# Turned data moves by another engine's DMA queue, its writes half a step later

## The chip, the cores and the metric

The kernel runs on one core of one Trainium2 chip. The metric is device time in microseconds; the kernel before takes 981.33 us (median of 3 runs, 980.38 to 981.82).

## The reference

A decoder trunk of two layers over 256 rows of 2048 columns, in float32. Each layer normalises its rows and multiplies them by one wide input matrix. Its columns are the queries, keys and values of two kinds of attention, the queries of a cross-attention into 256 memory rows, and a gate. The heads' outputs are multiplied by `silu(gate)` and sent through an output matrix; the input is added.

```python
h = rms_norm(x, norm_g) @ w_in
# layer 0: latent attention (8 heads), block attention (8 heads), memory attention (4 heads)
# layer 1: windowed attention with sinks (16 heads), dilated attention (6), memory attention (4)
y = jnp.concatenate([o_a, o_b, o_m], axis=-1) * jax.nn.silu(gate)
x = x + y @ w_out
```

A last RMS norm follows. With 256 rows every causal attention has two blocks of 128 queries.

## The kernel before, in words

Weights stream from memory in pieces of 128 partitions by up to 1024 elements (two row blocks of up to 512 columns). SyncE issues each piece's transfer into one of four `raw` tiles (line 329). ScalarE (ACT in the profile) writes its rounded part `hi` (L413) and VectorE (DVE) the rest `lo`; there are four buffers of each. TensorE (PE) makes each product in three matmuls, x-high by `hi`, x-high by `lo`, x-low by `hi` (L568 to L570), into a ring of four PSUM tiles. A piece is two half-steps of six matmuls. After each half-step `run_bg` (L475) advances all running background generators by one `yield`, so a `yield` means half a step later. A budget of VectorE work per half-step makes non-urgent generators skip a turn when it is spent. `ensure(i + AHEAD, True)` (L538) splits weights three pieces ahead of PE.

The instruction order on every engine's queue is fixed by this written order. An instruction that has to wait holds everything behind it on its engine.

Products come with rows on partitions, and attention needs them turned. This takes two steps. VectorE transposes blocks of 32 by 32; the rest of the turn is done by writing the tile to memory and reading it back with another order of blocks. Two generators do this:

- `g_land` (L652) for two `wide` tiles of projected data: rotary products on GpSimd where needed (L635 to L650), transposes into a `big` tile, write to `wd` (L667), read back (L671), then the parts are handed on.
- `g_turn` (L844) for a tile `P` of softmax probabilities: transpose, write to `pd` (L850), read back (L853). `g_causal_T` calls it for causal heads; `g_mem_T` (L883) runs two of them side by side for memory heads and counts their half-steps itself.

All these transfers stand on SyncE's queue, between the weights. A read waits for the landing of its write. Heads are taken from a queue at most every fourth half-step; each goes through split, scores, softmax, turn and the product with the values, and ends in a block of `y` (a high and a low part, `put_y`). The output projections (`wo00` to `wo13`) read these blocks; if one has not yet been written in the order, the background runs on until it has.

Of the kernel before, what the change touches and what calls it, by code (L numbers as in the profile page):

```python
# [206 lines left out]
def body(ctx, tc, xr, xT, memT, memr, wall, gains, fing, sinks, consts, out):  # L207
    nc = tc.nc
# [286 lines left out]
    def mmtile():  # L495
        if len(mmring) == 4:
            mmring.popleft()["force"]()
        mmring.append({})
        return ps.tile([128, 512], F32, name="mm", tag="mm", bufs=4), mmring[-1]
# [120 lines left out]
    def rope_rows(W, n, s0, s1, kind, t):  # L620

        tab, m, w, k = {"d": (cst, 8, 32, 128), "c": (lay, 4, 16, 128), "r": (lay, 8, 8, 256)}[kind]
        per = 32 // w
        if kind == "r":
            v = W[:, 0:128 * n].rearrange("p (b g h i) -> p b g h i", b=4, h=2, i=8)[:, :, 2 * s0:2 * s1]
            x1, x2 = v[:, :, :, 0], v[:, :, :, 1]
            g = 2 * (s1 - s0)
        else:
            v = W[:, 0:128 * n].rearrange("p (b g i) -> p b g i", b=4, i=w)[:, :, per * s0:per * s1, 0:m]
            g = per * (s1 - s0)  # L630
        cs, sn = (tab[:, 2 * k * i + k * t:2 * k * i + k * t + k].rearrange("p (b g i) -> p b g i", b=4, i=m)
                  [:, :, 0:g] for i in range(2))
        e = wtile("e", 512, 2)
        A, B = (e[:, 256 * i:256 * i + 4 * g * m].rearrange("p (b g i) -> p b g i", b=4, i=m) for i in range(2))
        mul, add = (lambda o, a, b: nc.gpsimd.tensor_tensor(o, a, b, op=OP.mult)), OP.add  # L635
        if kind == "r":
            e = wtile("e", 512, 2)
            C, E = (e[:, 256 * i:256 * i + 4 * g * m].rearrange("p (b g i) -> p b g i", b=4, i=m) for i in range(2))
            mul(A, x1, cs)
            mul(B, x2, sn)  # L640
            mul(C, x2, cs)
            mul(E, x1, sn)
            nc.gpsimd.tensor_tensor(x1, A, B, op=OP.subtract)
            nc.gpsimd.tensor_tensor(x2, C, E, op=OP.add)  # L644
        else:
            lo, hi = slice(0, m // 2), slice(m // 2, m)
            mul(A, v, cs)
            mul(B[:, :, :, lo], v[:, :, :, hi], sn[:, :, :, lo])
            mul(B[:, :, :, hi], v[:, :, :, lo], sn[:, :, :, hi])
            nc.gpsimd.tensor_tensor(v, A, B, op=OP.add)  # L650

    def g_land(Ws, n, ropes, done, L=None):  # L652

        for k in ropes:
            for t in range(2):
                rope_rows(Ws[t], n, *k, t)
            yield
        while L is None and not big.free:
            yield
        L = L or big.get()  # L660
        w = 128 * n
        for t in range(2):
            vec.transpose(L[:, w * t:w * t + w], Ws[t][:, 0:w])
            wide.put(Ws[t])
        yield
        d = wds.get()
        nc.sync.dma_start(d[0:256 * w].rearrange("(t p f) -> p t f", t=2, p=128),  # L667
                          L[:, 0:2 * w].rearrange("p (t f) -> p t f", t=2))
        for _ in range(5):
            yield  # L670
        nc.sync.dma_start(L[:, 0:2 * w].rearrange("p (g f) -> p g f", g=8),  # L671
                          d[0:256 * w].rearrange("(g p f) -> p g f", g=8, p=128))
        wds.put(d)
        for _ in range(6):
            yield
        land = {"t": L, "n": n}
        done([Part(land, s, n) for s in range(n)])

    def rows(kinds, done, r=None):


        n = len(kinds)
        n0 = n - kinds.count("g")
        ropes = [(kinds.index(k), kinds.rindex(k) + 1, k) for k in "dcr" if k in kinds]

        def evac(cur):
            Ws = []
            while len(wide.free) < 2:
                yield
            for t in range(2):  # L690
                Ws.append(wide.get())
                o = laid_out(Ws[t], n)
                src = rows_of(cur[t][:, 0:128 * n], n)
                if n0:
                    copy(o[:, :, 0:n0], src[:, :, 0:n0], r, t)
                if n0 < n:
                    nc.scalar.activation(o[:, :, n0:n], src[:, :, n0:n], AF.Tanh, scale=hx[:, t:t + 1])
            yield
            if n0 < n:
                for t in range(2):  # L700
                    o, src = laid_out(Ws[t], n), rows_of(cur[t][:, 0:128 * n], n)
                    vec.tensor_scalar(o[:, :, n0:n], o[:, :, n0:n], 1.0, hx[:, t:t + 1], op0=OP.add, op1=OP.mult)
                    vec.tensor_tensor(o[:, :, n0:n], o[:, :, n0:n], src[:, :, n0:n], op=OP.mult)
                yield
            launch(g_land(Ws, n, ropes, done))
        return evac
# [35 lines left out]
    def g_turn_x(x):  # L742

        for _ in range(4):
            yield
        while len(wide.free) < 2:
            yield
        Ws = [wide.get(), wide.get()]
        for t in range(2):
            copy(laid_out(Ws[t], 4), rows_of(x[:, 512 * t:512 * t + 512], 4), None, t)  # L750
            yield
        yield from g_land(Ws, 4, [], XT.append, x)
# [91 lines left out]
    def g_turn(P, W, n):  # L844

        vec.transpose(P[:, 0:128 * n], W)
        yield
        d = pds.get()
        c = d[0:128 * 128 * n]
        nc.sync.dma_start(c.rearrange("(p f) -> p f", p=128), P[:, 0:128 * n])  # L850
        for _ in range(4):
            yield
        nc.sync.dma_start(P[:, 0:128 * n].rearrange("p (a f) -> p a f", a=4),  # L853
                          c.rearrange("(a p f) -> p a f", a=4, p=128))
        pds.put(d)
        for _ in range(5):
            yield

    def g_causal_T(P, r, out):

        while not pw.free:
            yield
        w = pw.get()
        (_, p0), (_, p1) = cuts3(P)
        nc.scalar.activation(laid_out(w, 3)[:, :, 1:3], p1, AF.Copy, scale=r[:, 1:2])
        vec.tensor_scalar(laid_out(w, 3)[:, :, 0:1], p0, r[:, 0:1], None, op0=OP.mult)
        yield
        pw.put(w)
        yield from g_turn(P, w[:, 0:384], 3)
        while not ptp.free:  # L870
            yield
        PT = ptp.get()
        hi, lo = PT[:, 0:256], PT[:, 256:512]
        p = P.rearrange("p (a s j) -> p s a j", a=4, s=3)
        parts = [v.rearrange("p (s a j) -> p s a j", a=4, s=2) for v in (hi, lo)]
        out.append((hi, lo, p[:, 2], PT))
        nc.scalar.activation(parts[0], p[:, 0:2], AF.Copy)  # L877
        yield
        vec.tensor_tensor(parts[1], p[:, 0:2], parts[0].bitcast(F32), op=OP.subtract)
        yield  # L880
        yield

    def g_mem_T(P, r, out):  # L883

        gs = []
        for t in range(2):
            while not pw.free:
                yield
            w = pw.get()
            if t:  # L890
                nc.scalar.activation(w[:, 0:256], P[t][:, 0:256], AF.Copy, scale=r[:, 1:2])
            else:
                vec.tensor_scalar(w[:, 0:256], P[t][:, 0:256], r[:, 0:1], None, op0=OP.mult)
            yield
            pw.put(w)
            gs.append(g_turn(P[t], w[:, 0:256], 2))
            next(gs[t])
        for i in range(11):
            for g in gs:
                next(g, None)  # L900
            if i < 10:
                yield
        while not (ptp.free and spl.free):
            yield
        hi, lo = ptp.get(), spl.get()
        p = [P[t][:, 0:256].rearrange("p (a s j) -> p s a j", a=4, s=2) for t in range(2)]
        parts = [v.rearrange("p (s t a j) -> p t s a j", t=2, s=2, a=4) for v in (hi, lo)]
        out.append((hi, lo))
        for t in range(2):
            nc.scalar.activation(parts[0][:, t], p[t], AF.Copy)  # L910
        yield
        for t in range(2):
            vec.tensor_tensor(parts[1][:, t], p[t], parts[0][:, t].bitcast(F32), op=OP.subtract)
        yield
        yield
# [229 lines left out]
    w = spl.free[0][:, 0:128]  # L1145
    vec.memset(w.bitcast(F32), 1.0)
    for i in range(10):
        a = ones if i < 7 else w
# [370 lines left out]
    n = len(plan[-1][1].sizes)  # L1519
    for t in range(2):  # L1520
        p, slot = mmtile()
        slot["force"] = lambda: None
        for i in range(n):
            ensure(npieces - n + i)
            hi, lo = splits[npieces - n + i]
            for h in range(2):
                x = y1(2 * i + h)
                w = slice(512 * h, 512 * h + 512)
# [58 lines left out]
```

## Time and profile before

| what | value |
|---|---|
| median of 3 runs | 981.33 us |
| the profiled execution's own time | 980.83 us |
| its span (first to last instruction) | 979.0 us |
| PE busy | 960.9 us |
| ACT busy | 584.4 us |
| weights issued on SyncE, 512 KB each | 309 |
| landed data: writes and reads | 34 and 34 |
| probabilities: writes and reads | 54 and 54 |

Busy time of an engine does not include waiting, or issuing transfers. SyncE's queue appears as SPq, issues on ScalarE's queue as ACTq. Idle time of an engine that is not the bottleneck costs nothing, so the table is read together with the waits.

### The profile page before, as it was taken

To read this page: it belongs to the slowest core of one execution; us is meant where nothing else is said; L and a number is where in the kernel's file an instruction comes from. 1 tells how busy PE (TensorE), PEld (TensorE's weight loads), DVE (VectorE), ACT (ScalarE), POOL (GpSimd) and SP (SyncE) were. 2 spreads that over 40 slices of the span, in tenths; PEclk is the share of its full clock that TensorE was granted. 3 is DMA by queue.
4 is the path that set the end of the run, shared out by engine and by line. 5 is a ranking of instruction groups with operands and counts; after the bars stand their busy time and mean duration, and the time that the engine had idled before them with its cause. 6 is when DMAs were issued, how large, how long until landed. Compare 5 with 4: busy or idle time off the path is not lost.

```text
span 979.0 us, 13403 instructions
## 1 busy us (share of the span) xinstructions
PE 960.9 (98%) x4541; PEld 806.7 (82%) x4541; DVE 665.8 (68%) x1174; ACT 584.4 (60%) x1060; POOL 95.5 (10%) x159
## 2 busy tenths in 40 slices
PE   9999998999999999999999999999999999999996
PEld 7888876888888888888888888888888988898885
DVE  6746767777767656776656655867968767676743
ACT  7766645676756646665656544656757765655541
POOL 0001221000011011010000000010202111001410
PEclk9999998999999999999999999999999999999999
DMA  9888966997677787887987867696777878699832
GB/s 336 324 272 268 317 203 222 329 305 233 216 255 212 236 259 227 262 306 250 325 267 274 268 205 236 201 282 215 233 273 240 300 223 267 198 309 305 296 108 86
DMA packets 136692, 248.26 MB, mean 254 GB/s; under 512 B 38960, under 2 KB 80176, under 8 KB 136624
## 3 DMA queue, kind: packets, MB, share of 16 engines
q1 hardware_dynamic: 135904, 246.59, 76.7%
q10 hardware_dynamic: 720, 0.82, 0.2%
q8 instruction: 35, 0.57, 0.2%
q14 instruction: 33, 0.27, 0.1%
HBM read 216.05 MB, written 31.33 MB: 253 GB/s over the span
## 4 chain that ended last, share of the span: by engine, by line
PE 84%; DVE 0%; ACT 0%; POOL 0%; issue 0%; ACTq 0%; DVEq 0%
PE mm L568 25%; PE mm L569 25%; PE mm L570 25%; PE at L951 2%; PE at L942 2%; PE at L946 1%; PE mm L1533 1%; PE mm L1532 1%; PE mm L1531 1%; PE at L955 1%; PE at L1069 0%; DVE big L202 0%; ACT big L1505 0%; DVE st L202 0%; POOL wide L644 0%; ACT wide L616 0%
## 5 line engine op out<-in xcount | busy, mean ns | idle before, releaser
L202 DVE TENSOR_TENSOR lo<-raw,hi 128x1024 fp32r<-128x1024 f32 (+3 forms) x331 | 398.9, 1211 | 187.0 <-ACT hi L413 184.3
L413 ACT ACTIVATE hi<-raw 128x1024 fp32r<-128x1024 f32 (+3 forms) x329 | 339.8, 1038 | 221.7 <-PE mm L570 178.2
L568 PE MATMUL mm<-hi,bufB 128*128 128x512 f32 (+1 forms) x680 | 264.7, 389 | 6.1 <-ACT wide L616 5.5
L569 PE MATMUL mm<-lo,bufB 128*128 128x512 f32 (+1 forms) x680 | 262.8, 386 | 0.5 <-DVE lo L202 0.5
L570 PE MATMUL mm<-hi,bufB 128*128 128x512 f32 (+1 forms) x680 | 262.4, 386 | 0.0
L569 PE MATMUL mm<-lo,bufA 128*128 128x512 f32 (+1 forms) x620 | 239.3, 386 | 2.0 <-DVE lo L202 2.0
L568 PE MATMUL mm<-hi,bufA 128*128 128x512 f32 (+1 forms) x620 | 240.0, 387 | 0.1
L570 PE MATMUL mm<-hi,bufA 128*128 128x512 f32 (+1 forms) x620 | 238.8, 385 | 0.0
L568 PEld LDWEIGHTS mm<-hi,bufB 128*128 128x128 f32 x680 | 128.4, 189 | 32.1 <-ACT wide L616 6.6
L569 PEld LDWEIGHTS mm<-lo,bufB 128*128 128x128 f32 x680 | 128.5, 189 | 24.4 <-DVE lo L202 1.3
L570 PEld LDWEIGHTS mm<-hi,bufB 128*128 128x128 f32 x680 | 128.3, 189 | 24.7
L569 PEld LDWEIGHTS mm<-lo,bufA 128*128 128x128 f32 x620 | 116.5, 188 | 24.5 <-DVE lo L202 2.7
L570 PEld LDWEIGHTS mm<-hi,bufA 128*128 128x128 f32 x620 | 116.4, 188 | 23.2
L568 PEld LDWEIGHTS mm<-hi,bufA 128*128 128x128 f32 x620 | 116.4, 188 | 22.9 <-ACT wide L616 0.4
L635 POOL TENSOR_TENSOR e<-wide,cst 128x64 f32<-128x64 f32 (+2 forms) x48 | 22.3, 491 | 284.1 <-ACT wide L618 143.8
L202 DVE STREAM_TRANSPOSE big<-wide 128x512 f32<-128x512 f32 (+1 forms) x68 | 44.0, 680 | 4.9 <-POOL wide L644 3.9
L833 ACT ACTIVATE P<-P,st 128x128 f32<-128x128 f32 x76 | 33.9, 448 | 15.7 <-DVE st L202 15.4
L798 POOL TENSOR_TENSOR y<-qk,big 128x256 f32<-128x256 f32 x20 | 19.1, 969 | 198.6 <-DMA big<-wd 139.4
L202 DVE CUSTOM_DVE_ANT_1 P<-at,lay 128x128 f32<-128x128 f32 x76 | 24.1, 354 | 20.1 <-PE at L942 20.0
L635 POOL TENSOR_TENSOR e<-wide,lay 128x64 f32<-128x64 f32 (+4 forms) x34 | 18.8, 581 | 148.1 <-ACT wide L618 111.8
L585 ACT ACTIVATE spl<-big 128x128 fp32r<-128x128 f32 (+1 forms) x76 | 23.6, 354 | 15.2 <-PE at L942 15.2
L877 ACT ACTIVATE PT<-P 128x256 fp32r<-128x256 f32 x38 | 15.3, 411 | 25.6 <-PE at L951 23.4
(149 smaller groups left out, 734.9 us busy)
## 6 DMA issues: line engine op xcount, KB each, us to landing
raw<-in_wall SPq DMA_DIRECT2D x309, 512.0 KB, 4.6
wd<-big SPq DMA_DIRECT2D x32, 512.0 KB, 5.2
big<-wd SPq DMA_DIRECT2D x32, 512.0 KB, 6.1
pd<-P SPq DMA_DIRECT2D x38, 192.0 KB, 4.7
P<-pd SPq DMA_DIRECT2D x38, 192.0 KB, 4.6
raw<-in_wall SPq DMA_DIRECT2D x16, 384.0 KB, 4.1
raw<-in_wall SPq DMA_DIRECT2D x8, 320.0 KB, 3.6
big<-in_xT SPq DMA_DIRECT2D x4, 512.0 KB, 6.5
```

The source lines that it names most:

```text
L202: return f(out, *a, **k)
L413: nc.scalar.activation(hi[:, c], raw[:, c], AF.Copy)
L568: nc.tensor.matmul(p, xh, hi[:, w], start=kt == 0, stop=False, skip_group_check=True)
L569: nc.tensor.matmul(p, xh, lo[:, w], start=False, stop=False, skip_group_check=True)
L570: nc.tensor.matmul(p, xl, hi[:, w], start=False, stop=kt == g.kt - 1, skip_group_check=True)
L585: nc.scalar.activation(hi, src, AF.Copy)
L635: mul, add = (lambda o, a, b: nc.gpsimd.tensor_tensor(o, a, b, op=OP.mult)), OP.add
L798: nc.gpsimd.tensor_tensor(y.rearrange("p (g j) -> p g j", j=32), o.rearrange("p (g j) -> p g j", j=32), sg.v, op=OP.mult)
L833: nc.scalar.activation(P, rows_of(sc[:, c], 2) if mask is None else P, AF.Exp, bias=s[:, 2 + t:3 + t], scale=scale, accum_out=s[:, 4 + t:5 ...
L877: nc.scalar.activation(parts[0], p[:, 0:2], AF.Copy)
L942: nc.tensor.matmul(o, q[:, a + q0:a + q0 + 128], k[:, b:b + 256], start=first and i == 0, stop=last and i == 2, skip_group_check=True)
L951: nc.tensor.matmul(po, v[a], T[b], start=st and i == 0, stop=sp and i == 2, skip_group_check=True)
```

## The change

The four `dma_start` calls of `g_land` and `g_turn` go from SyncE's queue to ScalarE's. Each write comes one `yield` later; the number of yields between a write and its read stays five and four. `g_mem_T` drives its two turns for one half-step more. Weights, the inputs and the residual's transfers stay with SyncE.

```diff
             wide.put(Ws[t])
         yield
+        yield
         d = wds.get()
-        nc.sync.dma_start(d[0:256 * w].rearrange("(t p f) -> p t f", t=2, p=128),
+        nc.scalar.dma_start(d[0:256 * w].rearrange("(t p f) -> p t f", t=2, p=128),
                           L[:, 0:2 * w].rearrange("p (t f) -> p t f", t=2))
         for _ in range(5):
             yield
-        nc.sync.dma_start(L[:, 0:2 * w].rearrange("p (g f) -> p g f", g=8),
+        nc.scalar.dma_start(L[:, 0:2 * w].rearrange("p (g f) -> p g f", g=8),
                           d[0:256 * w].rearrange("(g p f) -> p g f", g=8, p=128))
...
         vec.transpose(P[:, 0:128 * n], W)
         yield
+        yield
         d = pds.get()
         c = d[0:128 * 128 * n]
-        nc.sync.dma_start(c.rearrange("(p f) -> p f", p=128), P[:, 0:128 * n])
+        nc.scalar.dma_start(c.rearrange("(p f) -> p f", p=128), P[:, 0:128 * n])
         for _ in range(4):
             yield
-        nc.sync.dma_start(P[:, 0:128 * n].rearrange("p (a f) -> p a f", a=4),
+        nc.scalar.dma_start(P[:, 0:128 * n].rearrange("p (a f) -> p a f", a=4),
                           c.rearrange("(a p f) -> p a f", a=4, p=128))
...
-        for i in range(11):
+        for i in range(12):
             for g in gs:
                 next(g, None)
-            if i < 10:
+            if i < 11:
                 yield
```

## Rows read from the trace of the kernel before

**Rows 1.** The page, part 1: busy us, share of the span, instructions.

```profile
PE 960.9 (98%) x4541; PEld 806.7 (82%) x4541; DVE 665.8 (68%) x1174; ACT 584.4 (60%) x1060; POOL 95.5 (10%) x159
```

**Rows 2.** Waits of PE: who waited for whom, us in total, times, longest.

```profile
PE mm L568 <- ACT wide L616: 5.5, 2, 2.9
PE mm L569 <- DVE lo L202: 2.4, 3, 1.2
```

**Rows 3.** Stretches of 25 us: busy per engine, PE's clock, DMA share, GB/s.

```profile
75.00:100.00 25.00, 22.93 (x129) 20.26 (x128) 16.82 (x35) 17.07 (x34) 4.38 (x8) 1.00 0.84 281
125.00:150.00 25.00, 22.30 (x99) 17.69 (x97) 15.84 (x20) 11.49 (x16) 8.49 (x11) 0.98 0.64 201
...
525.00:550.00 25.00, 25.00 (x112) 20.71 (x111) 19.08 (x33) 18.68 (x29) 0.70 (x1) 1.00 0.83 278
...
725.00:750.00 25.00, 25.00 (x127) 20.44 (x126) 20.45 (x67) 19.27 (x56) 7.24 (x18) 1.00 0.54 167
```

**Rows 4.** Timeline of PE: start us, duration, what, idle before and its releaser.

```profile
89.26 0.50 PE L569 MATMUL mm<-lo,bufA 128*128 128x512 f32 x1 [0.77 <-DVE lo L202]
...
93.51 0.50 PE L569 MATMUL mm<-lo,bufA 128*128 128x512 f32 x1 [1.19 <-DVE lo L202]
...
148.55 0.50 PE L568 MATMUL mm<-hi,bufB 128*128 128x512 f32 x1 [2.53 <-ACT wide L616]
...
152.78 0.80 PE L568 MATMUL mm<-hi,bufB 128*128 128x512 f32 x1 [2.95 <-ACT wide L616]
```

**Rows 5.** Groups by form: count | busy us, mean ns | idle before, releasers.

```profile
L413 ACT ACTIVATE hi<-raw 128x1024 fp32r<-128x1024 f32 x303 | 319.4, 1059 | 212.6 <-PE mm L570 170.8 <-DMA raw<-in_wall 25.6 <-issue 3.8
...
L202 DVE TENSOR_TENSOR lo<-raw,hi 128x1024 fp32r<-128x1024 f32 x303 | 374.3, 1241 | 176.1 <-ACT hi L413 175.2
```

**Rows 6.** Line 667, landing writes: issue ns min/median/max, then issue to landing.

```profile
L667 SPq DMA_DIRECT2D wd<-big x34: 370/427/1510, 81.8 to 881.6; - x34
...
DMA to landing us min/median/max: 4.1/5.2/9.0
```

**Rows 7.** The same of line 850, writes of P.

```profile
L850 SPq DMA_DIRECT2D pd<-P x54: 319/428/1294, 159.8 to 868.8; - x54
...
DMA to landing us min/median/max: 1.8/4.8/8.0
```

**Rows 8.** Issues of line 853 (reads of P), and ACT's own of line 1508.

```profile
L853 SPq DMA_DIRECT2D P<-pd x54: 362/398/1728, 169.5 to 876.9; - x54
...
L1508 ACTq DMA_DIRECT2D out<-big x4: 338/348/371, 961.9 to 975.1; - x4
```

**Rows 9.** Waits of SyncE's queue: us in total, times, longest us.

```profile
SPq L853 <- DMA pd<-P: 15.1, 13, 4.7
SPq L671 <- DMA wd<-big: 10.6, 8, 3.2
```

**Rows 10.** Timeline of SyncE's queue from 766 us.

```profile
767.76 0.90 SPq L850 DMA_DIRECT2D pd<-P  x2
...
772.68 0.95 SPq L853 DMA_DIRECT2D P<-pd  x2
773.73 0.45 SPq L329 DMA_DIRECT2D raw<-in_wall  x1
```

**Rows 11.** Timelines of ACT and DVE around 105 us.

```profile
101.14 2.97 ACT L413 ACTIVATE hi<-raw 128x1024 fp32r<-128x1024 f32 x3
...
104.65 0.58 DVE L202 STREAM_TRANSPOSE big<-wide 128x384 f32<-128x384 f32 x1 [0.41 <-POOL wide L644]
105.15 3.45 DVE L202 TENSOR_TENSOR lo<-raw,hi 128x1024 fp32r<-128x1024 f32 x3
```

**Rows 12.** Timeline of DVE: the last block of `y` in layer 0.

```profile
449.67 0.42 DVE L202 TENSOR_TENSOR y<-at,big 128x256 f32<-128x256 f32 x1 [0.93 <-PE at L955]
...
451.38 0.42 DVE L202 TENSOR_TENSOR bufB<-y,bufB 128x256 fp32r<-128x256 f32 x1
```

**Rows 13.** The page, part 3: DMA queues, packets, MB, share of 16 engines.

```profile
q10 hardware_dynamic: 720, 0.82, 0.2%
```

## The prediction

> **What bounds the kernel now.** I read the page's engine shares first: PE is busy 98% of the span, DVE 68%, ACT 60% [rows 1]. So the question is not how much work the other engines have but where PE stood still, and for whom. The waits of PE are the second view: outside the first microseconds it waited 5.5 us for ACT copies into `wide` and 2.4 us for a weight's low part `lo`, and for no weight transfer directly [rows 2]. The table of 25 us stretches says where: PE is busy all 25.00 us nearly everywhere, with 112 matmuls of 512 columns in a plain stretch, and loses time only at 75 to 100 us and from 125 us until shortly after 150 us, beside the start and the end [rows 3]. PE's timeline names the four pauses: 0.77 and 1.19 us for `lo` at 89 and 93 us, 2.53 and 2.95 us for the `wide` copies at 146 and 150 us [rows 4]. The second pair ends a chain of GpSimd's rotary products, a DVE transpose and an ACT copy in which no transfer stands.
>
> From 25.00 / 112 a matmul takes 0.223 us, so a half-step of the schedule (six matmuls) takes 1.34 us and a weight piece (twelve) 2.68 us. There are four `hi` buffers, and ACT's `hi` of piece i+3 starts when PE has finished piece i-1: that is what ACT mostly waits for, 170.8 us in all [rows 5]. PE then still has three pieces, 8.0 us, ahead of it. Less 1.06 us for `hi` and 1.24 us for `lo` [rows 5] a plain stretch has a lead of about 5.7 us. This is the cover for nearly everything below.
>
> **What leaves SP.** 34 + 34 transfers of landed data and 54 + 54 of probabilities, 176 issues. They took medians of 0.43 us (landing write), 0.43 us (write of P) and 0.40 us (read of P) [rows 6 to 8], so about 176 x 0.42 = 74 us of SP's queue. SP is also held at a read until its write has landed: 13 times, 15.1 us for P and 8 times, 10.6 us for landed data [rows 9]. Weights behind it are held too: after the two writes of P at 767.76 us the reads went out at 772.68 us and the next weight only at 773.73 us [rows 10]. All this goes. What is it worth? Only what PE waits for late weights, at most the 2.4 us of [rows 2], because everywhere else the lead swallowed it. And those pauses at 89 and 93 us come in a stretch where ACT and DVE themselves are late (the pieces of 320 columns pass PE faster than `hi` and `lo` are made), so I take 0 for it; ends 0 and -2.0 us (both pauses of [rows 4] gone).
>
> **What comes to ACT.** The four issues that ACT already makes took a median of 0.35 us [rows 8], the same kind on SP 0.43 with a longest of 1.73 us in [rows 8]. I take 0.42: 176 x 0.42 = 74 us. ACT then holds 584 + 74 = 658 us, 67% of the span. In the dense stretch 725 to 750 us ACT works 19.27 of 25 us [rows 3], and five of the moved issues fall there, 2.1 us, which fits. On PE: 0. Bounds: 0, and with 1.73 us for each, 304 us, ACT would be at 888 of 979 us; that dense stretch would need 27.9 of 25 us, 2.9 us too much, and with some four such stretches the upper end is +12 us. I take the value by its own issues (0.35), which lie far from the longest.
>
> **The new waits on ACT.** A write waits for DVE's transpose, and now comes one half-step later, so that DVE has 1.34 us more. A read waits for its write's landing: median 4.8 us (P) and 5.2 us (landed), longest 8.0 and 9.0 us [rows 6, 7]. The distance between the two stays four half-steps for P, 5.4 us, and five for landed data, 6.7 us. So the median read waits for nothing, and the worst 8.0 - 5.4 = 2.6 us or 9.0 - 6.7 = 2.3 us. Behind it on ACT stand the next `hi`, the exponentials and the splits for attention; behind those DVE's `lo`, and PE. The worst wait with its issue, 3.0 us, is under the lead of 5.7 us. Over the kernel I take 13 us of ACT, half of SP's 25.7 us [rows 9]; ends 0 and 25.7 us. On PE 0.
>
> One place has no such lead: 75 to 110 us. Six of the moved issues are there, 2.5 us. ACT has finished its run of three `hi` at 104.1 us, the transpose of the write that would now stand in that run ends at 105.23 us [rows 11]; ACT is held for up to 2 us and the third `hi` with it. DVE makes three `lo` in a row there until 108.6 us, so most of that is hidden. I take +0.3 us for the stretch, ends -2.0 (as above) and +3.
>
> **The half-step itself.** Each landing, and each turn of P, ends 1.34 us later, so a head that needs both is 2.7 us later. In the middle of a layer heads only shift against the weights, PE's work is the same. At the end of a layer the output projection reads the last block. Counted through the schedule, block 15 of layer 0 is complete in half-step 303 and first read in 305. Its chain in the trace: the last product's sum is taken up by DVE at 449.67 us, and `lo` is done, by way of ACT's `hi`, at 451.80 us [rows 12]: 2.1 us from the taking up to `lo`. PE has five half-steps, 6.7 us, between; with two fewer it has 4.0 us. So no pause: 0, ends 0 and +2 us (if a head slips two more half-steps). Layer 1's last block (13: complete in 619, read in 623) has more room.
>
> The budget that holds back DVE work per half-step is also dealt out anew around 140 us: the first memory head starts a half-step later, so the transposes that free `wide` may come a half-step sooner. That would shorten PE's pause, but the head's six score matmuls, 0.7 us, which PE now makes before the pause, move behind it. I take +0.1 us; ends -1.3 and +1.3 us, a half-step either way.
>
> **The sum.** 0 + 0 + 0 + 0.3 + 0 + 0.1 = +0.4 us. Against the profiled execution, whose span is 979.0 and whose own time is 980.83, that is 981.2 us. The runs shown have the median 981.33, half a microsecond higher, which would give 981.7. I predict 981.4 us, between the two: no change. What this measurement can tell from no change is 0.2%, 2 us.
>
> **Rivals.**
> *A, faster: SP's queue was the hidden brake.* For it: the weight held to 773.73 us in [rows 10], and the `lo` pauses. If those two pauses go (-2.0) and the chain at 146 us starts a half-step sooner (-1.3), 981.3 - 3.3 = 978.0 us. Against: PE did not wait after 773.73. The second queue is almost unused now, 0.82 MB [rows 13], so no row shows whether two queues move more. By the Trainium skill, page "DMA: Bandwidth & Descriptors", section "Issuing engines are not separate DMA queues", transfers from all issuing engines run interleaved on the same 16 DMA engines and a second issuer saves only sequencer time. By that rule A has nothing from bandwidth and keeps only the unblocked SP. Chance 0.12.
>
> *B, slower: a read held on ACT at 75 to 110 us or in front of a thin lead.* For it: PE waits for `lo` there already, six issues of 0.42 us are 2.5 us, and the held write above up to 2 us: +4.5, so 985.8 us. It decides from the point where ACT's hold exceeds the lead: 5.7 us in a plain stretch, about 0 at 80 to 95 us. Against: ACT is idle between its `hi` for over 200 us in all [rows 5]. The same page of the Trainium skill, section "Queues, rings and completion order", has each DMA engine take turns between queues packet by packet; by that the weights would be mixed with the turned data in place of queuing with it, and land later beside them. That lengthens B's stretch and no other. Chance 0.13.
>
> *C, slower: the later heads reach a layer's end late.* Two half-steps more than counted make the output projection wait for blocks 14 and 15: +1.5 to 2 us, 983.2 us. Against: 4.0 - 2.1 = 1.9 us remain above. Chance 0.05.
>
> **How the numbers follow.** Forecast 0.70 (its own range 979.6 to 983.2), A 0.12, B 0.13, C 0.05. A lies below 979.4 nearly whole, with 0.01 from the forecast's edge and a little of A left within: faster 0.11. B whole, half of C and 0.03 of the forecast's upper edge: slower 0.18. The same: 0.71. The range 979.3 to 984.3 leaves out A and the upper half of B, under 0.2.
>
> **What would show it.** Right: PE busy within 1 us of 960.9; its waits again the four pauses; ACT's busy time unchanged at 584 us with 176 issues of 0.35 to 0.45 us on its queue; SP's waits for landings gone; `hi` waiting less for PE and a little for DMAs. Step by step: an ACT issue far over 0.42 us, or reads held on ACT for over 26 us in all, refutes the cost of ACT; a PE wait for `lo` outside 75 to 110 us refutes the lead; a PE pause at the first matmuls on block 14 or 15 (450 to 460 us) refutes the half-step. The forecast fails if PE's total pause changes by more than 2 us.

## The result, and the profile after

The changed kernel took 988.06 us, median of 4 runs (987.15 to 988.76), beside 981.38 us for the kernel before on the same chip: ratio 1.0065, 95% interval 1.005 to 1.008. It is slower by 6.7 us where the forecast was no change (979.3 to 984.3).

The page of the changed kernel, part 1; the engines do what they did [rows 1]:

```profile
PE 964.4 (98%) x4541; PEld 807.9 (82%) x4541; DVE 668.0 (68%) x1173; ACT 583.8 (59%) x1061; POOL 95.6 (10%) x160
```

Its waits of PE, the answer to [rows 2]. The waits for `wide` have grown by 1.5 us, those for `lo` by 1.5, and a wait for DVE's work on `wide` is new:

```profile
PE mm L568 <- ACT wide L616: 7.0, 3, 3.2
PE mm L569 <- DVE lo L202: 3.9, 6, 1.2
PE mm L568 <- DVE wide L202: 1.3, 2, 1.1
```

Stretches of 25 us of the changed kernel, the answer to [rows 3], and two stretches that the prediction did not look at:

```profile
75.00:100.00 25.00, 22.79 (x128) 19.96 (x127) 17.12 (x35) 17.31 (x34) 3.63 (x8) 1.00 0.83 283
125.00:150.00 25.00, 22.13 (x100) 17.93 (x98) 16.37 (x18) 11.59 (x16) 9.73 (x12) 0.98 0.61 206
175.00:200.00 25.00, 21.55 (x88) 16.69 (x87) 17.41 (x27) 14.68 (x25) 0.00 (x0) 0.94 0.94 293
525.00:550.00 25.00, 25.00 (x112) 20.68 (x111) 18.94 (x33) 17.41 (x27) 0.70 (x1) 1.00 0.81 284
...
775.00:800.00 25.00, 23.36 (x120) 19.41 (x119) 17.50 (x39) 16.75 (x36) 0.00 (x0) 1.00 0.85 267
```

The same two stretches of the kernel before, where PE lost nothing:

```profile
175.00:200.00 25.00, 24.99 (x116) 20.56 (x115) 18.93 (x31) 16.55 (x29) 0.00 (x0) 1.00 1.02 333
775.00:800.00 25.00, 25.00 (x132) 21.27 (x132) 17.98 (x40) 17.06 (x36) 0.00 (x0) 1.00 0.88 287
```

To size it, I added up the intervals between matmuls beyond the usual (median) interval of the same shape. The sum rose from 19.7 to 27.7 us: by 5.7 us at 175 to 200 us and by 2.6 us at 775 to 800 us, and by -0.9 to +0.3 us in any other stretch. So the whole loss lies in two stretches, 50 us of 987.

PE's timeline names the pauses there (start, duration, what, idle before and its releaser):

```profile
190.41 0.47 PE L568 MATMUL mm<-hi,bufB 128*128 128x512 f32 x1 [1.09 <-DVE wide L202]
191.53 0.47 PE L568 MATMUL mm<-hi,bufB 128*128 128x512 f32 x1 [0.18 <-DVE wide L202]
195.96 0.50 PE L568 MATMUL mm<-hi,bufB 128*128 128x512 f32 x1 [2.13 <-ACT wide L616]
...
778.52 0.45 PE L569 MATMUL mm<-lo,bufB 128*128 128x384 f32 x1 [0.47 <-DVE lo L202]
...
791.48 0.50 PE L569 MATMUL mm<-lo,bufB 128*128 128x512 f32 x1 [0.72 <-DVE lo L202]
```

In the first stretch PE waits for evacuations of PSUM, in the second for weights. ACT's timeline of the changed kernel shows what they stood behind in the first (ACTq rows are issues; the bracket is the idle time before and its releaser):

```profile
171.81 2.77 ACTq L672 DMA_DIRECT2D big<-wd  x1
...
174.62 2.60 ACTq L668 DMA_DIRECT2D wd<-big  x1
177.26 1.06 ACT L413 ACTIVATE hi<-raw 128x1024 fp32r<-128x1024 f32 x1 [4.54 <-issue]
...
184.13 1.42 ACTq L852 DMA_DIRECT2D pd<-P  x2
185.60 1.06 ACT L413 ACTIVATE hi<-raw 128x1024 fp32r<-128x1024 f32 x1 [3.07 <-PE at L953]
185.68 2.60 ACTq L855 DMA_DIRECT2D P<-pd  x2
188.33 1.26 ACT L698 ACTIVATE wide<-mm,hx 128x512 f32<-128x512 f32 x2 [1.67 <-DMA raw<-in_wall]
...
195.31 1.19 ACT L616 ACTIVATE wide<-mm 128x512 f32<-128x512 f32 x2 [1.96 <-DVE big L202]
```

and the same two evacuations in the kernel before (the first is L697 there):

```profile
184.48 1.25 ACT L697 ACTIVATE wide<-mm,hx 128x512 f32<-128x512 f32 x2
190.84 1.19 ACT L616 ACTIVATE wide<-mm 128x512 f32<-128x512 f32 x2 [2.90 <-DVE big L202]
```

Between the two, DVE transposes the gate's tiles (DVE's timeline, before and then changed):

```profile
190.03 1.30 DVE L202 STREAM_TRANSPOSE big<-wide 128x512 f32<-128x512 f32 x2
```

```profile
194.57 1.30 DVE L202 STREAM_TRANSPOSE big<-wide 128x512 f32<-128x512 f32 x2
```

From 171 to 177 us two issues alone take 5.4 us, and `hi` goes out after 4.54 us of idle time. At 184 to 188 us four more issues stand right in front of the gate's evacuation, which comes at 188.33 in place of 184.48 us. DVE can finish its share of it, transpose, and so free `wide` only after that; the next evacuation comes at 195.31 in place of 190.84 us, 4.5 us later, and PE, out of PSUM tiles, stands for 1.09 + 0.18 + 2.13 = 3.4 us.

Two of those four issues were held for a weight, and not for a write of their own. The trace's semaphores show the write at 184.13 us held for 2.00 us until a weight had landed at 184.06 us, and the second read held for 1.81 us until another weight had landed at 187.80 us. ACT's timeline from 187 us on shows that read alone:

```profile
187.88 0.40 ACTq L855 DMA_DIRECT2D P<-pd  x1
```

So the release named at 188.33, a weight's landing, is right in substance: it let the read go, and the evacuation stood behind the read. Why an issue waits for a weight is told in the last section.

In the second stretch ACT is held at single issues:

```profile
773.19 0.33 ACTq L852 DMA_DIRECT2D pd<-P  x1
773.56 0.85 ACT L413 ACTIVATE hi<-raw 128x768 fp32r<-128x768 f32 x1 [4.03 <-DMA raw<-in_wall]
...
784.23 0.37 ACTq L672 DMA_DIRECT2D big<-wd  x1
784.64 0.31 ACT L928 ACTIVATE qf<-big 128x128 f32<-128x128 f32 x1 [2.84 <-DMA wd<-big]
```

Here both kinds of hold stand one after the other. The writes at 773.19 and 775.14 us were held for 3.99 and 1.12 us until weights had landed; two `hi` came late behind them, and PE's pause at 778.52 us followed. The read at 784.23 us had waited 3.5 us for its own write, issued at 776.04 and landed at 784.21 us; PE's pause at 791.48 us followed that. The pieces there have 384 columns, and `lo` is soon late.

### The profile page after: what moved, and what is told of

The parts are those of the page before. It is cut to its first block, busy times and chain, and to the rows that moved or that the text cites. A ratio compares the mean times of both kernels' runs of the same rounds, so it can differ in the third digit from the quotient of the medians.

```text
span 986.9 us, 13373 instructions
## 1 busy us (share of the span) xinstructions
PE 964.4 (98%) x4541; PEld 807.9 (82%) x4541; DVE 668.0 (68%) x1173; ACT 583.8 (59%) x1061; POOL 95.6 (10%) x160
## 3 DMA queue, kind: packets, MB, share of 16 engines
q10 hardware_dynamic: 81616, 55.10, 18.0%
## 4 chain that ended last, share of the span: by engine, by line
PE 77%; DMA 2%; DVE 2%; ACT 2%; issue 1%; ACTq 1%; POOL 0%; DVEq 0%; SPq 0%
PE mm L568 23%; PE mm L569 23%; PE mm L570 23%; PE at L953 2%; PE at L944 2%; DMA raw<-in_wall 2%; PE at L948 1%; DVE lo L202 1%; PE mm L1535 1%; PE mm L1533 1%; PE mm L1534 1%; ACT hi L413 1%; PE at L957 0%; DVE big L202 0%; DMA pd<-P 0%
## 5 line engine op out<-in xcount | busy, mean ns | idle before, releaser
L202 DVE TENSOR_TENSOR spl<-big,spl 128x128 fp32r<-128x128 f32 (+1 forms) x76 | 26.8, 391 | 3.0 <-ACT spl L585 2.8
```

Of the source, the lines that this page charges most:

```text
L202: return f(out, *a, **k)
```

## The experiments

The theories: **T1**, the loss comes from what the moved transfers do on ACT's queue (issues, and holds before them); **T2**, it comes from the later half-step, which shifts heads and evacuations into each other. Within T1, **L** (a read holds ACT until its own write has landed) against **R** (an issue holds ACT until the transfer eight issues earlier has landed), against a write's wait for DVE's transpose, and against the issues' own time. All ratios are to the kernel before, with 95% intervals. The kernel before was timed again beside each group of experiments, at 982.1 to 982.6 us, and their ratios go by that time, not by 981.38 us.

| run | on ACT | half-step later | ratio | interval |
|---|---|---|---|---|
| the change | all 176 | yes | 1.0065 | 1.005 to 1.008 |
| e1 | none | yes | 0.9993 | 0.9984 to 1.0002 |
| e2 | all | no | 1.0021 | 1.0012 to 1.003 |
| e3 | 68 of landed data | yes | 1.0020 | 1.0012 to 1.0029 |
| e4 | 108 of probabilities | yes | 1.0023 | 1.0014 to 1.0031 |
| e5 | 88 writes | yes | 0.9995 | 0.9986 to 1.0003 |
| e6 | 88 reads | yes | 1.0139 | 1.0125 to 1.0152 |
| e7 | all but the two stretches | yes | 1.0003 | 0.999 to 1.0016 |
| e8 | the two stretches alone | yes | 1.0062 | 1.0048 to 1.0075 |
| e9 | all, at the half-step's end | yes | 1.0066 | 1.0053 to 1.0079 |
| e10 | all, reads 2 later in the two stretches | yes | 1.0005 | 0.9996 to 1.0013 |
| e11 | 88 writes | no | 1.0020 | 1.0011 to 1.0029 |
| e12 | all, reads 1 nearer to writes | yes | 1.0035 | 1.0023 to 1.0047 |
| e13 | all but 10 reads | yes | 1.0019 | 1.0008 to 1.003 |
| e14 | 88 writes and those 10 reads | yes | 1.0044 | 1.0031 to 1.0058 |

**e1: the later half-step alone.**

```diff
-        nc.scalar.dma_start(...)   # four times, in g_land and g_turn
+        nc.sync.dma_start(...)
```

> All 176 transfers of turned data stay on SyncE; only the writes come one half-step later (and with them all that follows in each head). Theory T1 (the loss comes from issues and their holds on ACT's queue, which keep the hi copies and the evacuations of PSUM behind them late at 170 to 197 us and at 773 to 795 us): ACT has no issue to make, so 981.4 us, within 1.5 us of the kernel before, and no PE pause at 190 to 196 us. Rival T2 (the half-step itself shifts the heads and evacuations of the schedule into each other): the loss stays, 986 to 989 us, with PE pauses for the wide copies at 190 to 196 us although ACT issues nothing.

981.44 us, no difference. T2 falls as the cause by itself. The half-step is not free of effect: one pause of 1.13 us for `wide` appears at 192 us, and the stretch at 125 to 150 us loses 0.9 us less.

**e2: the queue alone.**

```diff
-        yield                      # the added one, in g_land and g_turn; 12 -> 11 in g_mem_T
```

> All 176 transfers on ACT's queue, the writes in the half-step where the kernel before has them. T1: the loss is there as in the changed kernel, 985 to 990 us; without the half-step the transposes of the writes are less often done, so ACT's waits for DVE in front of a landing write are longer than in the changed kernel. T2: 980 to 982.5 us, no pause at 190 to 196 us.

984.27 us: ACT's queue costs without the half-step too, but a third of the loss, not all of it. My range missed. The two parts work together, which neither theory had said.

**e3 and e4: one kind of transfer on ACT, the other on SyncE.**

```diff
-        nc.scalar.dma_start(c...)  and (P[...])     # e3: g_turn back
-        nc.scalar.dma_start(d...)  and (L[...])     # e4: g_land back
+        nc.sync.dma_start(...)
```

> Later writes everywhere; only the 68 transfers of landed data on ACT, the 108 of probabilities back on SyncE. In the changed kernel's run of seven issues at 168 to 177 us three are of landed data (0.46, 2.77 and 2.60 us), four of probabilities (1.53 and 1.00 us for two each). T1: the run falls to three issues, which also find fewer transfers ahead of them on their own queue; most of the loss goes: 981 to 984.5 us. If single long issues decide rather than the run, the 2.77 and 2.60 us stay and with them 985 to 987 us. T2: 986 to 989 us.

> Later writes everywhere; only the 108 transfers of probabilities on ACT, the 68 of landed data back on SyncE. T1: at 168 to 177 us four issues of 2.5 us in all remain on ACT, at 773 to 778 us some five; 981 to 984.5 us, and with the kernel that has landed data alone on ACT the two losses add up to less than the 6.7 us of the changed kernel, since a run of issues in which the later ones wait for the landings of the earlier ones costs more than its halves. T2: 986 to 989 us.

984.00 us, and 984.68 us, which is 0.2 us above its range; 0.20% and 0.23% add up to less than the 0.65% of both, as expected. The two stretches part cleanly. With landed data on ACT, PE loses at 775 to 800 us and little at 175 to 200 (less than in e1, where it is busy for 23.87 us); with probabilities the other way round (windows of e3, then of e4):

```profile
175.00:200.00 25.00, 24.22 (x112) 19.94 (x111) 19.56 (x33) 14.91 (x25) 0.00 (x0) 1.00 0.92 306
775.00:800.00 25.00, 23.63 (x119) 19.11 (x119) 18.23 (x39) 16.34 (x35) 0.00 (x0) 1.00 0.87 284
```

```profile
175.00:200.00 25.00, 22.55 (x96) 17.82 (x95) 17.35 (x27) 13.75 (x24) 0.00 (x0) 0.93 0.93 299
775.00:800.00 25.00, 25.00 (x133) 21.76 (x132) 19.48 (x40) 16.82 (x37) 0.00 (x0) 1.00 0.94 329
```

**e5 and e6: writes or reads on ACT, the others on SyncE.**

```diff
-        nc.scalar.dma_start(L[...])  and (P[...])   # e5: reads back
-        nc.scalar.dma_start(d...)    and (c...)     # e6: writes back
+        nc.sync.dma_start(...)
```

> Later writes everywhere; the 88 writes on ACT, the 88 reads on SyncE. Theory R (what holds ACT is that an issue waits until the transfer eight issues earlier, often a weight, has landed; in the changed kernel the longest such holds, 3.99, 2.09 and 2.00 us, stand in front of writes): most of the loss stays, 984.5 to 987.5 us. Theory L (what holds ACT is a read that waits for the landing of its own write): the loss goes, 981 to 982.5 us.

> Later writes everywhere; the 88 reads on ACT, the 88 writes on SyncE. Theory L: most of the loss stays, 984.5 to 987.5 us, with a hold of 2 us or more in front of a read at 168 to 180 us and at 775 to 785 us. Theory R: 981 to 983 us.

981.50 us with the writes on ACT, 995.77 us with the reads: twice the loss of the change, and above my range. I added up the holds, the time from when ACT's queue had sent off what stood ahead until the issue began: reads are held for about 86 us in e6 (32 of them for over 1 us), about 31 us in the change (12 over 1 us). So reads on ACT can cost much, as L has it. That L made the loss of the change is not shown by it: e6 loses most at 700 to 725 and at 875 to 900 us, where the changed kernel lost nothing, and in the two stretches of the change its PE is busy for 22.89 and 24.88 of 25 us, longer than in the change (21.55 and 23.36).

On R these two are no clean test: holds for an older transfer come to 11.1 us in the change, but only 1.1 us in e5 and 9.2 us in e6, since other transfers stand eight issues ahead. (The 2.09 us that the expectation of e5 counts among them lie within the issue ahead, which ran until 174.58 us.) The second stretch answers it better: e3 loses there with 0.4 us of such holds in the whole kernel, and e10 (below) loses nothing there with 9.0 us of them, one of 4.4 us at 770.7 us. So a loss there does not need R, and one long hold of R alone does not make one. But e3 is not L alone either: its `hi` stood behind a write that waited 3.5 us for DVE's transpose, and then behind a read held for 1.7 us. In the changed kernel 8.9 of the 11.1 us of R fall into the two stretches, beside 5.2 us in which reads there waited for their own writes, so both stand in front of its pauses; how much of the loss each makes is not shown. The clearest hold is in e6 (ACT's timeline, then PE's):

```profile
710.08 0.40 ACT L879 ACTIVATE PT<-P 128x256 fp32r<-128x256 f32 x1
715.17 5.12 ACTq L855 DMA_DIRECT2D P<-pd  x2
720.34 0.69 ACT L698 ACTIVATE wide<-mm,hx 128x512 f32<-128x512 f32 x1 [9.86 <-DMA big<-wd]
```

```profile
722.60 0.80 PE L568 MATMUL mm<-hi,bufB 128*128 128x512 f32 x1 [3.78 <-ACT hi L413]
724.72 0.79 PE L569 MATMUL mm<-lo,bufB 128*128 128x512 f32 x1 [1.32 <-DVE lo L202]
```

Two reads hold ACT from 710 to 720 us. The first goes at 715.17, when its write has landed (715.15); the second waits for its own write until 716.01 and then, as R has it, for an older read that lands at 719.90. Together that is more than the lead of 5.7 us, and PE stands for 3.78 + 1.32 = 5.1 us at a place where it lost nothing in the changed kernel.

**e7 and e8: by place.** In half-steps 108 to 130 and 513 to 548 the transfers go to SyncE (e7), or only those go to ACT (e8).

```diff
+    def q():
+        t = ctl["tick"]
+        return nc.sync if 108 <= t <= 130 or 513 <= t <= 548 else nc.scalar   # e8: the other way round
-        nc.scalar.dma_start(...)   # four times
+        q().dma_start(...)
```

> As the changed kernel, but the transfers written in half-steps 108 to 130 and 513 to 548 (about 160 to 193 us and 755 to 800 us, some 47 of the 176) go back to SyncE. Theory T1 in its local form (ACT's queue has room for an issue everywhere but in these two stretches): 981 to 982.5 us. Rival (the cost is spread, so much for every issue): 129/176 of the loss stays, 985.5 to 987 us.

> The other way round: only the transfers of those two stretches are on ACT, the other 129 on SyncE. Local form: 986 to 989 us, with the pauses of the changed kernel at 190 to 196 us and 778 to 795 us. Spread: 982.5 to 984 us.

981.56 and 988.93 us. The 42 transfers that the trace counts in the two stretches make the whole loss; the 134 others on ACT's queue cost nothing that can be measured, though one read among them was held for 7.4 us. The profile of e8, of the shortest of its six runs (985.13 us), shows pauses in the first of the two alone; at 775 to 800 us PE is busy all 25.00 us. That these transfers by themselves make the loss of the second stretch too is thus not seen.

**e9: issued at the end of the half-step.**

```diff
-        nc.scalar.dma_start(o, i)
+        tail.append((o, i))        # and at the end of run_bg:
+        while tail:
+            nc.scalar.dma_start(*tail.pop(0))
```

> The changed kernel, but the transfers that fall in a half-step are issued at its end, behind the hi copies, evacuations and attention work written in the same half-step, and not among them. Theory L: the holds stay and only what is written in the next half-steps stands behind them; a little of the loss goes, 984.5 to 988 us. If the work of the same half-step behind the issue is what PE waits for: 981 to 983.5 us.

989.21 us: a miss, nothing is gained. What stands behind an issue in its own half-step is not what matters; a hold is longer than a half-step and reaches the next ones.

**e10 and e12: the distance from write to read.**

```diff
+        far = 2 in half-steps 108 to 130 and 513 to 548, else 0     # e12: far = -1 everywhere
-        for _ in range(5):         # g_land; 4 in g_turn, 12 in g_mem_T
+        for _ in range(5 + far):
```

> The changed kernel, all 176 transfers on ACT, with two more half-steps between a write and its read in the two stretches alone (half-steps 108 to 130 and 513 to 548). Theory L (reads held on ACT until their write has landed make PE wait): the holds in front of reads there fall by up to 2 to 2.7 us each, and most of the loss goes, 981.5 to 984 us. If it is the issues' own time, the waits for transposes or the waits for older transfers: 986 to 989 us, or a little more, since the heads of these stretches come later still.

> The changed kernel with one half-step less between every write and its read, 1.0 to 1.34 us, which takes back the half-step by which the writes are later. Theory L: every read that is held is held by that much longer, and some that were not held are: 990 to 998 us. Theory T2 in a weaker form (later heads are part of the loss): 983 to 987 us, since the heads end where they did in the kernel before.

e10: 982.66 us, the loss is gone with every transfer still on ACT, though PE still stands for 1.7 us in the first stretch (in e1 for 1.1 us). Its two stretches:

```profile
175.00:200.00 25.00, 23.31 (x106) 19.02 (x105) 19.26 (x32) 14.77 (x25) 0.00 (x0) 1.00 0.97 310
775.00:800.00 25.00, 25.00 (x133) 21.55 (x132) 19.21 (x41) 16.81 (x36) 0.00 (x0) 1.00 0.90 298
```

In the second stretch the waits of reads for their own writes fell from 3.5 us to nothing, as L has it, and in the first from 1.7 us to nothing. The gate's evacuation comes at 186.19 us. But in the first stretch this is no clean test of the holds. In the profile of e13 (below) that evacuation comes at 186.18 us too, and yet the next one comes at 194.03 us, in e10 at 191.84 us. DVE's timelines show the difference, the transposes of the gate's tiles in e10 and then in e13:

```profile
191.04 1.30 DVE L202 STREAM_TRANSPOSE big<-wide 128x512 f32<-128x512 f32 x2
```

```profile
193.29 1.30 DVE L202 STREAM_TRANSPOSE big<-wide 128x512 f32<-128x512 f32 x2
```

In e10 one `lo` stands in front of them; in e13 and in the changed kernel two `lo`, two splits for attention and a part of `y`. The two half-steps more thus changed the written order on DVE as well.

e12 missed L's range: 985.49 us, less loss than the change although reads are held for about 59 us. So the sum of the holds does not set the loss. The time lies in the range of the weaker T2, later heads as a part of the loss, and e2, whose heads are not later either, also lost less than the change. Later heads alone cost nothing (e1); with all transfers on ACT's queue they seem to be a part of it. In e12 PE is busy 0.6 us less at 75 to 100 us and 1.5 us less at 175 to 200 us than before, and all 25.00 us at 775 to 800 us (what it lacks at 150 to 175 us, 1.7 us, it has gained at 125 to 150 us, 1.4 us): other places are hit.

**e11: the writes on ACT without the half-step**, as a version that could be the best.

```diff
-        nc.sync.dma_start(d...)  and (c...)         # in the kernel before
+        nc.scalar.dma_start(...)
```

> The kernel before with the 88 writes on ACT and the 88 reads on SyncE, no half-step added; written as the version that could be the best. Theory L: no read can hold ACT, and only waits for a transpose and the issues remain: 980 to 982.5 us. A gain over the kernel before would need SyncE's queue to have been a brake, which the kernel with all transfers on SyncE and later writes did not show.

984.05 us, a miss. Here no read is on ACT; the writes are held for about 70 us, in e5 for about 28 us, since a half-step earlier DVE's transposes are less often done. So with the writes alone on ACT the half-step is worth the 0.25% between e11 and e5. With all 176 transfers there it is the other way round: 1.0021 without it (e2), 1.0065 with it. And e2, with the reads on ACT too, is no slower than e11: in that schedule the reads add nothing. No version beat the kernel before by more than the measurement can tell.

**e13 and e14: ten reads.** The 8 reads of probabilities in half-steps 108 to 130 and the 2 of landed data in 513 to 548 go back to SyncE (e13), or are the only reads on ACT (e14).

```diff
-        nc.scalar.dma_start(L[...])
+        (nc.sync if 513 <= ctl["tick"] <= 548 else nc.scalar).dma_start(L[...])
-        nc.scalar.dma_start(P[...])
+        (nc.sync if 108 <= ctl["tick"] <= 130 else nc.scalar).dma_start(P[...])
```

> The changed kernel with 10 of its 176 transfers back on SyncE: the 8 reads of probabilities written in half-steps 108 to 130 and the 2 reads of landed data in half-steps 513 to 548. Theory L with these places: nearly all of the loss goes, 981.5 to 983.5 us. If the loss needs the whole load of ACT's queue (all issues of those stretches, writes too): 985 to 988 us.

> The other way round: all writes on ACT and of the reads only those 10; the 78 others on SyncE. Theory L with these places: most of the loss of the changed kernel is there, 985 to 989 us, with the pauses at 190 to 196 us and 778 to 795 us. If the loss needs the whole load: 981 to 984 us.

983.96 us, between the two ranges, and 986.35 us, in the range of L. Ten of the 176 transfers carry about two thirds of the loss (0.65% falls to 0.19% without them, and 0.44% is there with them and the writes alone). The rest goes with the other load of the queue. The thirds are rough, since the runs of one kernel spread with TensorE's clock: e14's six runs go from 984.50 us at a mean granted clock of 0.995, the profiled one, to 988.52 us at 0.992.

In the first stretch of e13 landed data and writes still hold ACT: its profile, of one of its longer runs (986.87 us), has a pause of 2.14 us at 194.7 us. In e14's profile the gate's evacuation comes at 188.31 us, as late as in the change, but behind another hold: a read that waited 2.70 us for its own write, landed at 187.00 us. At 775 to 800 us e14's PE is busy all 25.00 us, so the pauses expected there are missing. How the loss of the first stretch divides among the reads, the holds for older transfers, the long issues and the later heads is open, and so is why the reads cost nothing in the schedule of e2.

## Why the prediction was wrong

*What leaves SP: 0.* Right. With every transfer off SyncE at harmless places (e7) or merely later on it (e1) nothing is gained, so rival A fell. The Trainium skill, page "DMA: Bandwidth & Descriptors", section "Issuing engines are not separate DMA queues", says that a second issuer saves sequencer time alone. The trace agrees: ACT's queue moved 55.10 MB in place of 0.82 [rows 13], and all queues together ran at 252 GB/s, before at 254.

```profile
q10 hardware_dynamic: 81616, 55.10, 18.0%
```

*What comes to ACT: 74 us, on PE 0.* On ACT right in sum, 80.0 us, with medians as forecast [rows 6 to 8]; the issues of reads in the changed kernel (min, median, max ns, then issue to landing):

```profile
L672 ACTq DMA_DIRECT2D big<-wd x34: 366/367/2765, 89.2 to 896.9; - x34
...
DMA to landing us min/median/max: 3.9/5.8/10.7
```

```profile
L855 ACTq DMA_DIRECT2D P<-pd x54: 366/377/1900, 168.5 to 884.9; - x54
...
DMA to landing us min/median/max: 2.4/4.7/11.0
```

The zero on PE was argued from a mean rate per stretch. The long ones come together, where many transfers are under way: 5.4 us of ACT in two issues at 172 to 177 us.

*The new waits on ACT: 13 us, on PE 0.* This step failed, in three ways. First the size: about 31 us before reads, over my end of 25.7, and as much again before writes. A kind of wait was missing: 11.1 us in which an issue waited for a transfer eight issues earlier, 8.9 us of them in the two stretches. For the waits of reads I had taken four and five half-steps for 5.4 and 6.7 us; where pieces have 384 columns a half-step is 384/512 of 1.34, about 1.0 us, so that they are 4 and 5 us, and landings rose to 11.0 us. Second, "the worst wait with its issue, 3.0 us, is under the lead": a lead is spent by all holds that fall within it, not by the worst one, and holds come in rows. Third, and this is what made the larger loss: 5.7 us is the lead of `hi` and `lo`. ACT also evacuates PSUM, and there PE had far less: the evacuation at 195.31 us was 4.5 us late and cost 3.4 us, so the lead was about 1 us, an estimate from these rows. [Rows 2] named just that wait as the largest of the kernel before; I used it for the stretch at 146 us, and did not ask where else an evacuation would come behind the moved issues.

The Trainium skill, same page, section "Two DMAs through the same engine are not ordered", has it that the issuing engine must wait on the first transfer's semaphore before it issues a dependent one. The row at 784.23 us agrees. The wait thus moves with the read, to whatever engine issues it: what SyncE could wait out, ACT could not.

*The stretch at 75 to 110 us: +0.3.* Measured +0.3 us (75 to 100 us; nothing after). Rival B came nearest: ACT held in front of a thin lead was the mechanism, though not only by reads, and its price, 985.8 us, was near. Its two places were wrong, and I had weighed it at 0.13 because ACT is idle for over 200 us in all. That idle time lies elsewhere.

*The half-step: 0.* Right by itself (e1), but not beside the move: with all transfers on ACT's queue the ratio is 1.0021 without it (e2) and 1.0065 with it. No term of the sum had such a joint cost. *The budget near 140 us: +0.1.* 125 to 175 us changed by -0.6 us, within the bound.

*The sum* misses 5.7 us at 175 to 200 us and 2.6 us at 775 to 800 us. Of the 5.7 us, the three pauses are 3.9 us, counted from the start of one matmul to the start of the next, less the usual 0.23 us. The rest is TensorE's clock, for which the prediction has no term. Windows of the changed kernel and of e14 after almost the same pause, of 2.13 and 2.11 us, show it; clock is the third column from the end:

```profile
196.00:200.00 4.00, 4.00 (x11) 3.19 (x12) 3.30 (x4) 2.64 (x4) 0.00 (x0) 0.60 0.69 232
```

```profile
196.00:200.00 4.00, 4.00 (x21) 3.41 (x22) 3.57 (x5) 3.62 (x5) 0.00 (x0) 1.00 0.70 238
```

In the one the granted clock was 0.60, mostly the lower level of 1.2 GHz, in the other 1.00. The same twelve matmuls stand between the pause and the next attention product, in the changed kernel from 195.96 us on, in e14 from 195.94 us on:

```profile
200.40 0.28 PE L953 MATMUL at<-PT,vr 128*128 128x256 f32 x1
```

```profile
195.94 0.50 PE L568 MATMUL mm<-hi,bufB 128*128 128x512 f32 x1 [2.11 <-ACT wide L616]
...
198.80 0.28 PE L953 MATMUL at<-PT,vr 128*128 128x256 f32 x1
```

They took 4.44 us in the one and 2.86 us in the other, so the clock cost 1.6 us, and 3.9 + 1.6 = 5.5 of the 5.7 us.

## What to carry to other kernels

Before a dependent transfer is moved to an engine that also computes, list everything that engine does behind it, and give each its own lead: here a copy that frees PSUM had about 1 us where weights had 5.7 us. Add up all holds within one lead, with the landing times of the busiest stretch and not the medians. Count every kind of hold: a read waits for its write's landing, a write for the work whose result it stores, and either can wait for an older transfer of the other queue, as it did here. On SyncE, which has nothing else to do, all 176 transfers cost nothing (e1). The writes alone cost nothing on ACT with the half-step (e5) and 0.20% without it (e11).

## What the hardware showed that was not expected

- An issue on ACT took a median of 0.37 us, and 2.77 and 2.60 us in a row at 172 to 177 us, with seven transfers under way.
- The program has eight completion semaphores for the transfers of both queues, used in turn: before an issue, its queue waits until the transfer that had this semaphore last, eight issues earlier, has landed, whichever queue that was on. The write at 773.19 us was held for 4.0 us until a weight issued on SyncE's queue at 766.69 us had landed, at 773.11. In the changed kernel ACT was so held 6 times by weights, 10.0 us in all; on SyncE before, twice, 1.8 us.
- After equal pauses of 2.1 us, ended at 196 us, the granted clock fell in one run (0.60) and not in another (1.00), which was worth 1.6 us. Shortly before, PE had stood for 1.09 and 0.18 us in the first and for 0.73 and 0.19 us in the second.
